# Output projection as seven block products for eight, and a gating summed in PSUM: one Trainium2 core

## The chip, the core and the metric

One of the eight cores of a Trainium2 chip runs the kernel. A core has a matrix engine (TensorE, PE in the profile, with PEld for its weight loads), a vector engine (VectorE, DVE), a scalar engine (ScalarE, ACT), a general engine (GpSimd, POOL) and a sync engine (SyncE, SP), which here issues every transfer between DRAM and the on-chip memory SBUF. TensorE writes its sums into PSUM, eight banks of 512 float32 columns per partition; VectorE and ScalarE read them there. Each engine works through its own instructions in a fixed order and waits on semaphores for the others.

The metric is the device time of one execution in microseconds, the median of several runs. The profiled execution is one more run, with the hardware profiler on.

## What is computed

One layer of a streaming encoder, for 2048 prompt tokens and 32 sample tokens (2080 rows of 1024 float32 numbers). Cut to what matters:

```python
h = jnp.einsum('bsd,de->bse', x, w_in)
u, v, ga, bv, bg, gb = jnp.split(h, ...)          # six pieces of 512 columns
u = jax.nn.gelu(u, approximate=False)
v = layer_norm(jax.nn.gelu(v, approximate=False), a_ln_g, a_ln_b)
y_a = u * spatial_gating(v, a_ws, a_bias) * jax.nn.silu(ga)
a = bv * jax.nn.sigmoid(bg)
c, new_hist = depthwise_causal_conv(conv_hist, a, b_conv_w, b_conv_b)   # 31 taps
y_b = jax.nn.silu(layer_norm(c, b_ln_g, b_ln_b)) * jax.nn.silu(gb)
y = jnp.einsum('bse,ed->bsd', jnp.concatenate([y_a, y_b], axis=-1), w_out)
x_new = layer_norm(ALPHA * x + y, post_ln_g, post_ln_b)
```

Spatial gating mixes positions: for each of 8 heads and each chunk of 128 tokens, a lower triangular 128 x 128 matrix is multiplied with the 64 channels of that head in v, and a bias is added.

## The kernel before

**Numbers in two parts.** TensorE is fed with fp32r, a 4-byte type that keeps fewer bits than float32. Every operand is therefore split: `hi` is the value cast to fp32r (ScalarE) and `lo` is the value minus `hi` (a subtraction on VectorE, `tt`, or on GpSimd, `gtt`). A product is then three matmuls, hi·hi, hi·lo and lo·hi, added in PSUM.

**Stages.** The tokens form four groups of 512; group 1 holds the 32 sample tokens as well. Two passes `p` of two groups each run over the input projection in steps: first `v` of the pass's first group (`mm_v`, lines 293 to 295), then `bg` and `bv`, `v` of the second group, `u`, `ga` and `gb` (`mm_f`, lines 266 and 269). A schedule clock `T0` counts 1 for a `v` step and 2 for the others, 192 units in all (`TEND`). A list planner orders each engine's instructions by priority; `when(t)` sets the priority of what follows, `at(t, ...)` hangs work on the step that begins at unit t. Weights come step by step: `load_w` four steps ahead, `split_w` up to three steps ahead, its low half on GpSimd.

**Spatial gating** (`spat`, lines 496 to 514). For two chunks of v at once, the 128 columns of two chunks' 64 channels are the weights, and `wt`, which holds the high and low part of a head's matrix side by side (256 columns), is the moving operand. Two matmuls (lines 507 and 508) with the high and the low part of v add into a PSUM area of 2 x 128 columns per head. The two halves are then added: ScalarE copies the first to `S` (line 513), VectorE adds the second (line 514, helper line 58). Each group takes 32 such matmuls and the sample 16, 144 in all.

**Convolution and its layer norm.** 31 taps on VectorE (helper line 61, tile `c`), two channel blocks at a time; `ln_chain` follows with column sums on TensorE (`colsum`, lines 378 and 379). For the last group they run into the output phase. The gated results y go to DRAM (`Yd`).

**Output projection.** `load_wo` reads the 16 tiles of w_out (8 k-blocks x 2 halves of 512 columns) and splits them, low parts on VectorE. Then come units of 256 tokens in the order 0, 1, 2, 3, sample, 4, 5, 6, 7. `load_y` reads y of a unit and splits it (ScalarE line 611, GpSimd), `load_r` reads x. `o_tile` makes a tile of 128 tokens: for each half of 512 columns 8 k-blocks x 3 matmuls (lines 659 to 661), then VectorE computes ALPHA·x + product from PSUM and takes statistics; the last tile's second half is cut into two pieces of 256. `finish` normalises: aggregate, a power on GpSimd, four multiplications with addition on VectorE, and the store. `o_sample` treats the 32 sample tokens with high and low part stacked as 64 weight columns.

Of the kernel before, what the change touches and what calls it, by code (L numbers as in the profile page):

```python
# [40 lines left out]
def hymba_step_kernel(ctx, tc, xT, xn, xs_n, wall, wsT, abias, vecs, avec, post, cache,  # L41
                      y_p, y_s, nc_p, nc_s, nav):

# [187 lines left out]
    def setup_hi():  # L231
        nc.scalar.copy(wt[:, :, 0, :], setup["wm"])
# [141 lines left out]
    def colsum(g, hl, nm):  # L374
        r = []
        for b, (c0, w) in enumerate(blocks(g)):
            p = ps.tile([P, W], F32, name=f"{nm}{g}_{b}", tag="c", bufs=2)
# [1 line left out]
            nc.tensor.matmul(p[:, :w], ones, hl[1][:, c0 : c0 + w], start=False, stop=True)
# [83 lines left out]
    def ev_v(g, res):  # L463
# [32 lines left out]
        def spat(u, pr, two):  # L496
# [3 lines left out]
            if (u, pr, two) == (0, 0, 0):  # L500
                S[g] = sb.tile([P, 4, WMAX], F32, name=f"S{g}", tag="S", bufs=2)
            p = bank(f"sp{g}_{u}_{pr}_{two}")
            for q in range(2):
# [3 lines left out]
                nc.tensor.matmul(o, hi, wt[:m, h], start=True, stop=False)  # L507
                nc.tensor.matmul(o, lo, wt[:m, h], start=False, stop=True)  # L508
            p4 = p.rearrange("p (q a b) -> p q a b", q=2, a=2)
            for j, (_, c0, _) in enumerate(ch):  # L510
                r = slice(64 * j, 64 * j + 64)
                d = S[g][64 * two : 64 * two + 64, pr : pr + 2, c0 : c0 + m]
                nc.scalar.copy(d, p4[r, :, 0, :m])  # L513
# [311 lines left out]
```

## Time and profile before

| what | value |
|---|---|
| time, median of 3 runs | 783.99 us (783.91 to 786.16) |
| the profiled execution, whole | 786.06 us |
| its span, first to last instruction | 784.2 us |
| TensorE busy | 764.3 us, 97% |
| VectorE busy | 627.7 us, 80% |
| ScalarE busy | 274.0 us, 35% |
| GpSimd busy | 260.5 us, 33% |
| transfers | 79.12 MB, mean 101 GB/s |
| matmuls and weight loads | 3799 of each |

How to read the profile: a row of the groups view has the line, the engine, the operation, the tile written and those read, the shapes (for a matmul rows*columns of the weights, then partitions x columns of the moving operand), the count, then busy microseconds and mean nanoseconds of one, then the engine's idle time just before and what ended it. A helper's line stands for all that call it: line 58 is every `tt`, 61 every `stt`, 64 every `gtt`, 67 every activation. A row of the timeline has start and length in us, and in brackets the idle time before. Matmuls overlap, so the slot of one is the distance between two starts, not its length.

### The profile page before, as it was taken

How to read it: one execution, taken by the hardware profiler on the slowest of the kernel's cores; microseconds unless marked ns; L12 is line 12 of the kernel's file. 1: busy time of each engine (PE TensorE's matmuls, PEld its weight loads, DVE VectorE, ACT ScalarE, POOL GpSimd, SP SyncE). 2: the span in 40 equal slices, each digit the busy share in tenths (PEclk: the TensorE clock that was granted, in tenths of full speed). 3: DMA queues.
4: the chain of work that ended last, by engine and by line, in shares of the span. 5: the costliest groups of instructions: out<-in, count | busy, mean ns of one | idle time of the engine just before them, and what ended most of it. 6: DMA issues, size and time to landing. Idle time of an engine off the chain costs nothing.

```text
span 784.2 us, 10387 instructions
## 1 busy us (share of the span) xinstructions
PE 764.3 (97%) x3799; PEld 640.6 (82%) x3799; DVE 627.7 (80%) x986; ACT 274.0 (35%) x499; POOL 260.5 (33%) x204
## 2 busy tenths in 40 slices
PE   8999999999999999999899999999989999899996
PEld 6799998799889998888688888888878888688885
DVE  5339999882799999965999996899999987955455
ACT  6562222353562234376312343551350124011100
POOL 2652122343313339451213343221213322243320
PEclk9999999999999999999999999999999999999998
DMA  9621112211125327411211311124542244354411
GB/s 296 234 67 43 41 41 52 87 53 42 37 65 172 123 81 210 114 40 43 82 53 58 95 40 54 41 94 161 176 146 70 82 150 152 141 182 161 147 54 54
DMA packets 45474, 79.12 MB, mean 101 GB/s; under 512 B 7152, under 2 KB 16496, under 8 KB 45296
## 3 DMA queue, kind: packets, MB, share of 16 engines
q1 hardware_dynamic: 45424, 78.46, 31.3%
q8 instruction: 30, 0.49, 0.3%
q14 instruction: 20, 0.16, 0.1%
HBM read 61.21 MB, written 17.23 MB: 100 GB/s over the span
## 4 chain that ended last, share of the span: by engine, by line
PE 92%; DVE 3%; ACT 2%; DMA 1%; issue 1%; POOL 0%; SPq 0%; DVEq 0%; ACTq 0%; POOLq 0%
PE f L266 37%; PE f L269 18%; PE o L659 8%; PE o L660 8%; PE o L661 8%; PE t L295 4%; PE t L294 4%; PE t L293 4%; PE sp L507 1%; DVE r L61 1%; PE sp L508 1%; DMA xr<-in_xT_dram 0%; DVE ls L406 0%; ACT A L67 0%; DVE gb L58 0%
## 5 line engine op out<-in xcount | busy, mean ns | idle before, releaser
L266 PE MATMUL f<-xs,wh 128*128 128x512 f32 (+1 forms) x1600 | 369.6, 352 | 5.3 <-DVE S L58 3.3
L61 DVE SCALAR_TENSOR_TENSOR c<-A,vec,c 128x512 f32<-128x512 f32 x464 | 319.3, 749 | 2.5 <-ACT c L67 0.6
L266 PEld LDWEIGHTS f<-xs,wh 128*128 128x128 f32 x1600 | 271.7, 189 | 48.0 <-issue 5.9
L64 POOL TENSOR_TENSOR wl<-wr,wh 128x512 fp32r<-128x512 f32 x104 | 138.6, 1335 | 320.5 <-ACT wh L145 311.1
L269 PE MATMUL f<-xs,wl 128*128 128x512 f32 (+1 forms) x800 | 214.2, 351 | 0.0
L269 PEld LDWEIGHTS f<-xs,wl 128*128 128x128 f32 x800 | 140.7, 188 | 20.4 <-issue 0.2
L145 ACT CAST wh<-wr 128x512 fp32r<-128x512 f32 x112 | 69.2, 620 | 237.1 <-PE f L266 139.5
L659 PE MATMUL o<-wo,yh 128*128 128x512 f32 (+1 forms) x264 | 103.9, 394 | 4.7 <-ACT yh L611 4.7
L660 PE MATMUL o<-wo,yh 128*128 128x512 f32 (+1 forms) x264 | 103.4, 392 | 0.0
L661 PE MATMUL o<-wo,yl 128*128 128x512 f32 (+1 forms) x264 | 97.5, 387 | 0.0
L64 POOL TENSOR_TENSOR yl<-yr,yh 128x512 fp32r<-128x512 f32 x32 | 44.9, 1411 | 83.4 <-ACT yh L611 82.2
L659 PEld LDWEIGHTS o<-wo,yh 128*128 128x128 f32 x264 | 50.6, 192 | 16.5 <-ACT yh L611 5.6
L660 PEld LDWEIGHTS o<-wo,yh 128*128 128x128 f32 x264 | 50.7, 192 | 10.7
L661 PEld LDWEIGHTS o<-wo,yl 128*128 128x128 f32 x264 | 50.0, 189 | 11.0
L611 ACT CAST yh<-yr 128x512 fp32r<-128x512 f32 x32 | 19.6, 621 | 106.9 <-PE o L660 81.4
L61 DVE SCALAR_TENSOR_TENSOR r<-r,o 128x512 f32<-128x512 f32 (+1 forms) x33 | 21.6, 666 | 42.1 <-PE o L661 42.1
L58 DVE TENSOR_TENSOR S<-sp,S 64x256 f32<-64x256 f32 (+1 forms) x68 | 27.8, 409 | 26.9 <-ACT S L513 25.2
L294 PE MATMUL t<-wl,xs 128*128 128x512 f32 x128 | 49.3, 395 | 0.0
L293 PE MATMUL t<-wh,xs 128*128 128x512 f32 x128 | 47.7, 394 | 1.4 <-ACT xs L185 1.4
L295 PE MATMUL t<-wh,xs 128*128 128x512 f32 x128 | 48.4, 397 | 0.0
L64 POOL TENSOR_TENSOR xs<-xr,xs 128x512 fp32r<-128x512 f32 (+1 forms) x24 | 31.4, 1323 | 28.3 <-ACT xs L165 28.3
L64 POOL TENSOR_TENSOR or<-or,mhalf 128x1 f32<-128x1 f32 x16 | 16.0, 1000 | 72.4 <-DVE or L639 72.2
(109 smaller groups left out, 677.7 us busy)
## 6 DMA issues: line engine op xcount, KB each, us to landing
wr<-in_wall_dram SPq DMA_DIRECT2D x112, 256.0 KB, 2.6
yr<-yd SPq DMA_DIRECT2D x64, 128.0 KB, 2.2
r<-in_xn_dram SPq DMA_DIRECT2D x16, 512.0 KB, 4.5
out_dram<-r SPq DMA_DIRECT2D x15, 512.0 KB, 2.6
xr<-in_xT_dram SPq DMA_DIRECT2D x23, 256.0 KB, 4.1
wor<-in_wall_dram SPq DMA_DIRECT2D x16, 256.0 KB, 2.8
yd<-S SPq DMA_DIRECT2D x12, 256.0 KB, 2.6
yd<-gb SPq DMA_DIRECT2D x12, 256.0 KB, 2.1
```

The costliest lines, as they stand in the source:

```text
L58: nc.vector.tensor_tensor(out, a, b, op=op)
L61: nc.vector.scalar_tensor_tensor(out, a, s, b, op0=op0, op1=op1)
L64: nc.gpsimd.tensor_tensor(out, a, b, op=op)
L145: nc.scalar.copy(hi, r)
L266: nc.tensor.matmul(pt[b][:, :w], hk, xsp[g, k][:, part, c0 : c0 + w], start=(k == 0 and part == 0), stop=False)
L269: nc.tensor.matmul(pt[b][:, :w], lk, xsp[g, k][:, 0, c0 : c0 + w], start=False, stop=(k == NK - 1))
L293: nc.tensor.matmul(pt[t][:m], hi[:, c0 : c0 + m], wh, start=st, stop=False)
L294: nc.tensor.matmul(pt[t][:m], hi[:, c0 : c0 + m], wl, start=False, stop=False)
L295: nc.tensor.matmul(pt[t][:m], lo[:, c0 : c0 + m], wh, start=False, stop=en)
L659: nc.tensor.matmul(p, hi, wh, start=(k == 0), stop=False)
L660: nc.tensor.matmul(p, hi, wl, start=False, stop=False)
L661: nc.tensor.matmul(p, lo, wh, start=False, stop=(k == NK - 1))
```

## The change

Three things change.

1. **Spatial gating in PSUM.** `wt` becomes two tiles, high and low. `spat` now takes four heads of one kind (`two`) into one bank of 4 x 128 columns and adds three matmuls of 128 columns per head there: hi·high, hi·low, lo·high. ScalarE copies the result to `S`; the addition on VectorE is gone, as is the fourth product lo·low.

```diff
-        def spat(u, pr, two):
+        def spat(u, two):
...
-                o = p[:w, 256 * q : 256 * q + 256]
-                nc.tensor.matmul(o, hi, wt[:m, h], start=True, stop=False)
-                nc.tensor.matmul(o, lo, wt[:m, h], start=False, stop=True)
...
+                o = p[:w, P * pr : P * pr + P]
+                for m3, (l, r) in enumerate(((hi, 0), (hi, 1), (lo, 0))):
+                    nc.tensor.matmul(o, l, wt[r][:m, h], start=(pr + m3 == 0), stop=(m3 == 2),
+                                     skip_group_check=True)
...
-                nc.scalar.copy(d, p4[r, :, 0, :m])
-                tt(d, p4[r, :, 1, :m], d, ADD)
+                nc.scalar.copy(S[g][64 * two : 64 * two + 64, :, c0 : c0 + m], p3[r, :, :m])
```

2. **Sums of w_out blocks.** With w_out as 2 x 2 blocks of 512 x 512 (B11, B12, B21, B22), `wo_sums` makes T1 = B12 - B11, T3 = B22 - B12, T2 = B22 - T1 and T4 = B21 - T2 on GpSimd, splits them and stores both parts in DRAM (`Td`). It is called eight times during the first pass, at units 24, 30, 36, 42, 70, 74, 78 and 82.

```diff
+    def wo_sums(kk, c):
...
+                nc.sync.dma_start(b[i, dh], wo_rows(4 * i + kk, dh)[:, cs])
+        gtt(b[0, 0], b[0, 1], b[0, 0], SUB)
+        gtt(b[0, 1], b[1, 1], b[0, 1], SUB)
+        gtt(b[1, 1], b[1, 1], b[0, 0], SUB)
+        gtt(b[1, 0], b[1, 0], b[1, 1], SUB)
+        for j, (n, t) in enumerate(((1, b[0, 0]), (3, b[0, 1]), (2, b[1, 1]), (4, b[1, 0]))):
+            hl = sb.tile([P, 2, 256], F32R, name=f"to{kk}{c}_{n}", tag="v" + "hl"[j % 2], bufs=VB)
+            nc.scalar.copy(hl[:, 0], t)
+            gtt(hl[:, 1], t, f(hl[:, 0]), SUB)
+            nc.sync.dma_start(Td[n, kk][:, :, cs], f(hl))
```

3. **The output phase.** Its order is now 0, 1, sample, 2, 3, 4, 5, 6, 7. Units 0 and 1 and the sample are computed as before. Units 2 to 7 (1536 tokens) use Winograd's form of Strassen's scheme on 2 x 2 blocks: the two tiles of 128 tokens and the two halves of k give A11, A12, A21, A22, VectorE makes S1 = A21 + A22, S2 = S1 - A11, S3 = A11 - A21 and S4 = A12 - S2, and seven products of 12 matmuls replace eight. Partial sums stay in three PSUM banks, A, B and C, that are read after each product and added to by a later one. `mm` chains all these matmuls in the order written. Every low part of y (`YDVE = ()`) and every second one of w_out is made on GpSimd. The layer norm of the last group (`late`) is cut into six stages that are put between the products. `load_y(0)` comes 13 units before the end of the input projection, w_out is loaded half by half, and T1 to T4 come back through `load_t`.

```diff
+    def mm(out, l, r, start, stop):
+        with tc.issue_after(order["mm"].ins):
+            order["mm"] = nc.tensor.matmul(out, l, r, start=start, stop=stop, skip_group_check=True)
...
+        (tt if k % 2 else gtt)(t[:, 1, :W], r, f(t[:, 0, :W]), SUB)
...
+    PRODUCTS = [("A11", "B11", "A"), ("A12", "B21", "B"), ("S2", "T2", "A"), ("S3", "T3", "C"),
+                ("S1", "T1", "A"), ("A22", "T4", "C"), ("S4", "B22", "A")]
...
+    def y_block(u, n):
...
+            tt(s1, a21, a22, ADD)
+            tt(a21, a11, a21, SUB)
+            tt(a11, s1, a11, SUB)
+            tt(a12, a12, a11, SUB)
...
+        nc.scalar.copy(hl[0], raw)
+        (tt if n in YDVE else gtt)(hl[1], raw, f(hl[0]), SUB)
...
+    def o_product(u, j, t0, final):
...
+        parts = [slice(0, 256), slice(256, W)] if final and j == 6 else [slice(0, W)]
+        for n, cs in enumerate(parts):
...
+            for kk in range(4):
+                wh, wl = wo[wn, kk]
+                for m, (l, w) in enumerate(((hi, wh), (hi, wl), (lo, wh))):
+                    mm(q, l[:, kk], w[:, cs], opens and kk + m == 0, kk == 3 and m == 2)
...
+            if j in (0, 2, 3, 6):
+                stt(r[t][:, c], r[t][:, c], ALPHA, q)
+            else:
+                tt(r[t][:, c], r[t][:, c], q, ADD)
...
+            if j in (1, 4, 5, 6):
+                nc.vector.bn_stats(ost[t][:, dh + n, :], r[t][:, c])
```

`finish` has a second form for all prompt tiles but the last: a small VectorE step for minus mean times scale, then ScalarE, VectorE and GpSimd one after another over the whole row of 1024.

```diff
+        if parts["out"] == [slice(0, D)] and m == P:
+            nm = sb.tile([P, 1], F32, name=f"on{tag}", tag="on1", bufs=4)
+            stt(nm, mv[:, 0:1], -1.0, r1, op0=MUL, op1=MUL)
+            act(r, r, AF.Identity, bias=nm, scale=r1)
+            tt(r, r, pgb[:, 0], MUL)
+            gtt(r, r, pgb[:, 1], ADD)
```

In the planning of the Strassen units, blocks of y are prepared up to five products ahead:

```diff
+            while ready < len(blocks_y) and ready - len(used) < 5:
+                v, n = blocks_y[ready]
+                if (v, "A11") not in yraw:
+                    when(t - 11 + j)
+                    load_yraw(v)
+                when(t + j - 8)
+                y_block(v, n)
+                ready += 1
+            o_product(u, j, t + j, u == units[-1])
+            stages(t + j, LATE.get((u, j), 0))
```

More of the change, by code (lines that the diff above doesn't have):

```diff
@@ L437, in run @@
                 lambda: (sw(0, 1, 2, 3), gates()),
-            )
+            ]
+            if g == 3:
+                late.extend(fns)
+            else:
+                chain(h, *fns)
         run()
@@ L546, in ev_v @@
         )
-        units = [(u, pr, two) for u in range(3 if five else 2) for pr in (0, 2) for two in range(2)]
+        units = [(u, two) for u in range(3 if five else 2) for two in range(2)]
         for j, a in enumerate(units):
-            at(h + 6 + 2 * j // 2 + (4 if a[0] else 0), lambda a=a: spat(*a))
-        at(h + 6 + len(units) + 4, spat_affine)
+            at(h + 6 + 2 * j + (4 if a[0] else 0), lambda a=a: spat(*a))
+        at(h + 6 + 2 * len(units) + 4, spat_affine)
     def gated(g, e, i):
@@ L677, in o_sample @@
                 for x in range(2):
-                    nc.tensor.matmul(p[: 2 * NS], both, wo[k, dh][:, x, :W],
-                                     start=(k == 0 and x == 0), stop=(k == NK - 1 and x == 1))
+                    mm(p[: 2 * NS], both, wo[f"B{1 + k // 4}{1 + dh}", k % 4][x],
+                       k == 0 and x == 0, k == NK - 1 and x == 1)
             s = slice(W * dh, W * dh + W)
             stt(r[:, s], r[:, s], ALPHA, p[:NS])
-            e = work(f"ro{dh}")[:NS, :W]
+            e = sb.tile([P, W], F32, name=f"ro{dh}", tag="wr", bufs=4)[:NS]
             nc.scalar.copy(e, p[NS : 2 * NS])
@@ new lines, in hymba_step_kernel @@
+    YDVE = ()
+    def o_product(u, j, t0, final):
+        yn, wn, grp = PRODUCTS[j]
+        if j in (0, 1, 3):
+            psum[grp] = bank(f"o{grp}{u}")
+        if j == 0:
+            for t in range(2):
+                ost[t] = sb.tile([P, 3, 6], F32, name=f"ost{u}_{t}", tag="ost", bufs=4)
+        hi, lo = Y[u, yn]
+        r = R[u]
+        parts = [slice(0, 256), slice(256, W)] if final and j == 6 else [slice(0, W)]
+        for n, cs in enumerate(parts):
+            when(t0 + n / 2)
+            q = psum[grp][:, cs]
+            opens = j in (0, 1, 3)
+            for kk in range(4):
+                wh, wl = wo[wn, kk]
+                for m, (l, w) in enumerate(((hi, wh), (hi, wl), (lo, wh))):
+                    mm(q, l[:, kk], w[:, cs], opens and kk + m == 0, kk == 3 and m == 2)
+            when(t0 - 12)
+            t, dh = ((0, 0), (0, 0), (1, 0), (1, 1), (1, 1), (1, 0), (0, 1))[j]
+            c = slice(W * dh + cs.start, W * dh + cs.stop)
+            if j in (0, 2, 3, 6):
+                stt(r[t][:, c], r[t][:, c], ALPHA, q)
+            else:
+                tt(r[t][:, c], r[t][:, c], q, ADD)
+            when(t0 + 1 + n / 2)
+            if j in (1, 4, 5, 6):
+                nc.vector.bn_stats(ost[t][:, dh + n, :], r[t][:, c])
+        if j in (5, 6):
+            split = final and j == 6
+            out = [slice(0, W), slice(W, W + W // 2), slice(W + W // 2, D)] if split else [slice(0, D)]
+            row = 256 * u + P * t
+            finish(r[t], P, {"st": ost[t], "n": 2 + split, "out": out}, y_p[row : row + P],
+                   f"{u}_{t}")
@@ L699, in hymba_step_kernel @@
     at(30, lambda: nc.sync.dma_start(pgb, bcast(post, P, 2 * D)))
+    for j in range(8):
+        at((24 + 6 * j) if j < 4 else (54 + 4 * j), lambda j=j: after_w(wo_sums, j // 2, j % 2))
     for k in range(8):
```

178 lines of the change are left out of this document (127 added, 51 removed).

## The prediction

> **What bounds the kernel now.** I read the page first (span, busy shares, chain), then the groups with shapes kept apart, the waits of TensorE, the windows around them, and the timeline at both ends of the output projection.
>
> ```profile
> span 784.2 us, 10387 instructions
> PE 764.3 (97%) x3799; PEld 640.6 (82%) x3799; DVE 627.7 (80%) x986; ACT 274.0 (35%) x499; POOL 260.5 (33%) x204
> ...
> GB/s 296 234 67 43 41 41 52 87 53 42 37 65 172 123 81 210 114 40 43 82 53 58 95 40 54 41 94 161 176 146 70 82 150 152 141 182 161 147 54 54
> ```
>
> TensorE (PE) is busy 764 of 784 us, so a matmul more or less is a gain or loss of its full slot, wherever it stands. The 20 us that it isn't busy are a start, an end, and three stops:
>
> ```profile
> 376.64 1.16 PE L266 MATMUL f<-xs,wh 128*128 128x512 f32 x2 [3.34 <-DVE S L58]
> 584.88 0.80 PE L659 MATMUL o<-wo,yh 128*128 128x512 f32 x1 [1.96 <-ACT yh L611]
> 686.36 0.50 PE L659 MATMUL o<-wo,yh 128*128 128x512 f32 x1 [2.75 <-ACT yh L611]
> 370.00:380.00 10.00, 6.66 (x27) 5.39 (x26) 9.78 (x17) 6.02 (x15) 1.67 (x1) 0.83 0.36 138
> 390.00:400.00 10.00, 10.00 (x44) 8.11 (x44) 8.68 (x14) 2.78 (x4) 2.43 (x2) 1.00 0.21 52
> 585.00:595.00 10.00, 10.00 (x37) 8.16 (x38) 10.00 (x15) 2.42 (x5) 5.33 (x3) 0.83 0.40 124
> 686.00:696.00 10.00, 9.64 (x35) 7.76 (x36) 6.16 (x7) 2.49 (x5) 7.93 (x6) 0.83 0.70 225
> ```
>
> The bracket is the idle time and who ended it; in the window rows PE's time and matmul count come first, the granted clock third from the end. After each stop the clock is 0.83 over ten microseconds: 37 and 35 matmuls where 44 fit, 7 and about 8 slots lost. So the stops cost 3.34+1.5 (estimate, by the other two), 1.96+1.6 and 2.75+1.9: 13 us in all.
>
> **The slots.** From the chain of waits, and the first and last of 48 matmuls of 256 columns in the last tile:
>
> ```profile
> 630.73 0.46 PE o L661 x2
> 571.82 0.93 PE f L266 x4
> 771.22 0.28 PE L659 MATMUL o<-wo,yh 128*128 128x256 f32 x1
> 776.76 0.28 PE L661 MATMUL o<-wo,yl 128*128 128x256 f32 x1
> L507 PEld LDWEIGHTS sp<-wt,vh 128*128 128x128 f32 x64 | 11.1, 188 | 1.0 <-DVE A L58 0.3
> L507 PEld LDWEIGHTS sp<-wt,vh 32*64 32x64 f32 x8 | 0.9, 129 | 0.6
> ```
>
> 512 columns take 0.231 us (0.93/4), 256 columns 5.54/47 = 0.118. A weight load of 128 columns lasts 59 ns longer than one of 64, so 0.92 ns a column, and 128 columns occupy the loader about 0.118 us (an estimate from these two rows). That equals the 256-column slot.
>
> **Strassen: removed matmuls.** A block product is 128 tokens x 512 x 512 for both token halves: 4 k-blocks x 3 (hi·hi, hi·lo, lo·hi) = 12 matmuls. Six units of 256 tokens go from 8 to 7 products: 6 x 12 = 72 matmuls of 0.231 = **-16.6 us**. Units 0 and 1 and the sample keep theirs. With no bound hiding it, the gain is whole if nothing else becomes late.
>
> **Spatial gating: 144 wide matmuls become 216 narrow ones.** Before, 4 groups x 32 + 16 for the sample, 256 columns: 144 x 0.118 = 17.0 us. After, 4 x 48 + 24 = 216 of 128 columns, each with its own weight load. No row shows a moving operand under 256 columns in this 4-byte type. Lower end: by columns alone 0.231/4 = 0.058, 12.5 us (-4.5). Upper end: the dearest matmul of the trace, 0.231, 49.9 us (+32.9). I take 0.118, the weight load, which must pass once per matmul: 25.5, so **+8.5 us**.
>
> The Trainium skill, "TensorE: Matmul & The Clock Gate", section "Back-to-back issue gap", gives about 81 ns per matmul at 128 columns for a stream with weight loads. By it the edit costs 17.5 - 17.0 = +0.5, not +8.5 (an estimate from that page); no run here shows it yet.
>
> **What the gating takes from VectorE and ScalarE.**
>
> ```profile
> L58 DVE TENSOR_TENSOR S<-sp,S 64x256 f32<-64x256 f32 x64 | 27.0, 422 | 26.8 <-ACT S L513 25.2
> L513 ACT COPY S<-sp 64x256 f32<-64x256 f32 x64 | 23.4, 366 | 20.0 <-PE sp L508 12.6 <-DVE S L58 5.3
> L379 PE MATMUL mu<-lr,ones x5: 287/389/394, 203.2 to 633.1; 128*128 128x512 f32 x3, 128*128 128x272 f32 x2
> ```
>
> All 27 us of adds go, and ScalarE does 32 copies of twice the width for 64. VectorE isn't the bound, so this is worth only what it unblocks: the 376 us stop waits for just such an add (a PSUM bank held by it). I book **-4.8**; 0 if another VectorE step holds the next bank instead (VectorE is busy 9.8 of those 10 us).
>
> **Sums of w_out blocks.**
>
> ```profile
> L64 POOL TENSOR_TENSOR wl<-wr,wh 128x512 fp32r<-128x512 f32 x104 | 138.6, 1335 | 320.5 <-ACT wh L145 311.1 <-ACT S L513 4.8 <-ACT ls L67 2.4
> 50.00:100.00 50.00, 49.94 (x320) 45.57 (x319) 43.60 (x72) 16.05 (x36) 12.87 (x11) 1.00 0.14 43
> 200.00:250.00 50.00, 50.00 (x303) 43.35 (x302) 46.58 (x71) 24.68 (x46) 13.37 (x10) 1.00 0.24 75
> ```
>
> Eight calls, each 8 GpSimd (POOL) steps of 256 columns (half of 1.335, an estimate), 4 casts, 4 loads and 4 stores: 43 us of GpSimd, 64 DMAs on SP's queue. They lie where GpSimd has about 37 of 50 us free. Queued behind them are the low halves of w, split up to three steps (about 17 us) ahead, and behind a store that waits for its sum, the loads of w, four steps ahead. Cost **0**; if a call blocks longer than that lead, PE waits microsecond for microsecond.
>
> **The start of the output phase.** y of unit 0 is loaded 13 schedule units early, so the 585 us stop loses its named cause. But the order of matmuls is now fixed, and the eight w_out tiles of the first half are needed one per 0.69 us; half their low parts move to GpSimd at 1.335 instead of 0.719. I book half, **-1.8**. The 686 us stop stood behind the sample, which now comes after unit 1: **-4.6**, 0 at worst. The layer norm of the last group has its sums at fixed places in PE's order, about 52 us in (224 matmuls of units 0, 1 and the sample), 635 us; the last such sum started at 633.1 before (the third row gives first and last start), with more VectorE work ahead of them. Cost 0; if the convolution is later, PE stands.
>
> **The hand-over.** The sums come back as 16 tiles of 512 KB, 8 MB. T3 is issued after unit 0's matmuls (96 x 0.231 = 22 us in), T2 after unit 1's (44 us), T1 waits for the sample's last use of B12, and T1 is needed at product 4 of unit 2 (52 + 4 x 2.77 = 63 us). So from 44 to 63 us T2 and T1 (4 MB), unit 1's stores and y of unit 3 (1 MB each) move: 6 MB in 19 us, 316 GB/s, where the highest slice of the page has 296. At 296 they take 20.3 us, 1 to 2 more. Cost 0 to 10 (T4's 2 MB in the same stretch); I take **+2**, the rate's own answer.
>
> **The steady Strassen units.** PE needs 84 x 0.231 = 19.4 us per unit.
>
> ```profile
> L64 POOL TENSOR_TENSOR yl<-yr,yh 128x512 fp32r<-128x512 f32 x32 | 44.9, 1411 | 83.4 <-ACT yh L611 82.2
> L64 POOL TENSOR_TENSOR or<-or,mhalf 128x1 f32<-128x1 f32 x16 | 16.0, 1000 | 72.4 <-DVE or L639 72.2
> L58 DVE TENSOR_TENSOR wo<-wor,wo 128x512 fp32r<-128x512 f32 x16 | 11.3, 719 | 0.1
> L61 DVE SCALAR_TENSOR_TENSOR r<-r,o 128x512 f32<-128x512 f32 x31 | 20.8, 682 | 38.8 <-PE o L661 38.8
> L664 DVE BATCH_NORM_STATS2 ost<-r 128x6 f32<-128x512 f32 x31 | 21.0, 688 | 0.6
> L58 DVE TENSOR_TENSOR wt<-wm,wt 128x1024 fp32r<-128x1024 f32 x1 | 1.2, 1226 | 0.1
> L232 ACT CAST wt<-wm 128x1024 fp32r<-128x1024 f32 x1 | 1.0, 1045 | 0.0
> ```
>
> VectorE: 7 reads of PSUM x 0.68, 4 statistics x 0.69, 4 block sums x 0.72, 2 multiplies x 1.23, about 1 of small steps: 13.9 us, hidden. GpSimd: 7 splits x 1.41, 2 powers x 1.0, 2 adds of 1024 x 2.67 (twice 1.335): **17.2 of 19.4**, hidden with little room. New waits: three PSUM banks are each reopened two products after they are read, so VectorE has one product, 2.77 us, to read a bank; behind PE's wait stands its whole fixed order. 0 to 6 us over six units; I take **+3**.
>
> **The tail.**
>
> ```profile
> 777.08 0.42 DVE L61 SCALAR_TENSOR_TENSOR r<-r,o 128x256 f32<-128x256 f32 x1 [1.96 <-PE o L661]
> 779.66 1.53 DVE L61 SCALAR_TENSOR_TENSOR r<-r,or,pgb 128x512 f32<-128x512 f32 x3
> out_dram<-r SPq DMA_DIRECT2D x15, 512.0 KB, 2.6
> ```
>
> The last tile keeps its short end: matmuls done at 777.0, span over 7.2 later. But the other half of unit 7, done one product (2.8 us) before, ends by ScalarE 1.05, VectorE 1.23 and GpSimd 2.67 after its statistics (0.68+0.69+0.35) and power (1.0), then its store (about 2.6): 10.3 plus hand-offs, against VectorE's work for the last tile. Between 0 and +5; **+2.5**.
>
> **Sum:** -16.6 + 8.5 - 4.8 - 1.8 - 4.6 + 2 + 3 + 2.5 = **-11.8 us**. The profiled run took 786.06 us for a span of 784.2; the median shown is 783.99. The span would be 772.4, the same run 774.3; from the median I forecast **772.2 us**.
>
> **Rivals.**
> *Narrow matmuls are dear (slower).* Place: 216 gating matmuls. If one costs as much as a 512-column one, 216 x (0.231-0.118) = +24.4: 796.6 us. It decides from 0.173 us each (0.118 + 11.8/216). For it: the shapes of the trace stop at 256 columns, so no row denies it. Against: from 512 to 256 columns the slot halves exactly (0.231, 0.118), with no sign of a dearer rate.
> *Narrow matmuls are cheap.* At 0.058, 13.0 less: 759.2. For it: wide slots go by columns exactly. Against: the loader's 0.118. By the 81 ns of the Trainium skill's page cited above, "TensorE: Matmul & The Clock Gate", it would be 764.2 (an estimate).
> *GpSimd sets the pace of the Strassen units.* Between power and add of one tile stand a VectorE step, ScalarE and VectorE (0.16+1.05+1.23, some 2.9 with hand-offs). If GpSimd idles there twice a unit, it needs 23.0 us against 19.4: 21.6 over six units, less a lead of up to five blocks (13.9): 7.7 to 21.6. With 10, most of the lead being there: 782, no change.
> The Trainium skill's "GPSIMD Engine Reference", section 3.1, says to keep elementwise work on VectorE, measured 1.96 times faster. The trace agrees (1411 against 719 ns, 1.96), and this rule speaks against giving GpSimd the splits.
> *It doesn't do what it says* (the planner puts other work between, so PE stops at each product) is the upper end of the +3.
>
> **How the numbers follow.** Forecast (764 to 780) 0.50; cheap 0.13 (755 to 764); GpSimd's pace 0.17 (780 to 794); dear 0.20 (from 784 up). About 0.3% is what a measurement of this kernel can tell from no change: faster means under 781.6, slower over 786.4. Faster 0.50 + 0.13 + 0.06 of GpSimd's case = 0.69; same 0.06; slower 0.20 + 0.05 = 0.25. The range 758 to 796 leaves out the lowest part of the cheap case (0.04) and the upper half of the dear one (0.10). The forecast's own range is 764 to 780.
>
> **What would show it.** The start-to-start of the new gating matmuls: 0.118, 0.058 or 0.231. The matmul count of the output phase, 728 for 800. No idle of PE named after S at the first stop. PE's clock at 1.00 through units 2 to 7, and a unit in 19.4 us; if longer, the releaser (POOL: its pace; DVE r: the banks; DMA t: the sums late). I am wrong if the gating slot is over 0.17, or if the last product of a unit waits for a GpSimd split.

## The result

The changed kernel took 805.06 us (median of 4 runs, 802.8 to 805.96), beside 785.08 us (783.91 to 787.47) for the kernel before on the same chip: a ratio of 1.0246, 95% interval 1.0211 to 1.0281. It is **slower by 2.5%**; 772.2 us was forecast, so the sign was wrong, and the time lies above the range.

The first lines of the page after:

```profile
span 801.1 us, 10703 instructions
PE 765.4 (96%) x3787; PEld 637.6 (80%) x3787; DVE 636.7 (79%) x937; ACT 309.6 (39%) x531; POOL 385.1 (48%) x309
```

TensorE is as busy as before (765.4 for 764.3 us), with fewer wide matmuls: what it saved came back in narrow matmuls and in slower ones. The span grew by 16.9 us. GpSimd (POOL) has 125 us more work. Where the time went is read from windows, before and then after. Columns: stretch and its length, then busy time (and count) of PE, PEld, DVE, ACT and POOL, granted clock, DMA share, GB/s.

```profile
210.00:220.00 10.00, 10.00 (x55) 7.18 (x53) 9.18 (x17) 5.76 (x12) 3.50 (x2) 1.00 0.12 34
220.00:230.00 10.00, 10.00 (x63) 8.91 (x63) 9.94 (x14) 5.92 (x10) 1.29 (x1) 1.00 0.28 83
230.00:240.00 10.00, 10.00 (x64) 9.10 (x64) 10.00 (x15) 4.76 (x9) 2.58 (x2) 1.00 0.31 105
...
650.00:777.00 127.00, 124.25 (x554) 99.84 (x552) 81.60 (x124) 17.25 (x27) 36.12 (x30) 0.99 0.36 125
```

```profile
210.00:220.00 10.00, 10.00 (x44) 6.94 (x43) 8.58 (x11) 3.39 (x7) 1.82 (x2) 0.86 0.14 34
220.00:230.00 10.00, 10.00 (x43) 6.77 (x42) 7.67 (x8) 6.71 (x11) 1.72 (x2) 0.84 0.15 52
230.00:240.00 10.00, 10.00 (x53) 9.09 (x52) 10.00 (x18) 1.53 (x4) 7.45 (x5) 0.79 0.34 106
...
595.00:647.00 52.00, 52.00 (x226) 40.40 (x225) 50.40 (x84) 13.11 (x20) 21.71 (x16) 1.00 0.52 167
647.00:790.00 143.00, 124.61 (x519) 98.90 (x518) 119.12 (x157) 46.12 (x63) 93.01 (x62) 0.95 0.41 143
```

Two places. **The front:** from 210 to 240 us PE is busy without a gap, yet makes 140 matmuls for 182, and its clock, 1.00 before, is 0.79 to 0.86. The first matmul of the output phase starts at 594.95 us for 584.88: +10.1. **The Strassen units**, 647 to 790 us: their 504 matmuls of 0.231 us need 116.4 us and take 143. The output phase as a whole takes 195.2 us with 728 matmuls, 191.9 with 800 before: +3.3, where -16.6 and the old stops' end should show. **The tail:** last matmul to the end of the span 10.9 us for 7.4: +3.5. The three make the 16.9.

PE's timeline after shows what each place is made of (start, length, in brackets the idle time before and who ended it):

```profile
52.09 0.28 PE L541 MATMUL sp<-wth,vh 128*128 128x128 f32 x1
...
52.98 0.28 PE L541 MATMUL sp<-wth,vl 128*128 128x128 f32 x1
...
213.91 0.27 PE L541 MATMUL sp<-wth,vl 32*64 32x128 f32 x1
214.11 0.50 PE L271 MATMUL f<-xs,wl 128*128 128x512 f32 x1
...
214.74 0.39 PE L271 MATMUL f<-xs,wl 128*128 128x272 f32 x1
215.06 0.27 PE L541 MATMUL sp<-wtl,vh 32*64 32x128 f32 x1
...
319.50 0.79 PE L295 MATMUL t<-wh,xs 128*128 128x512 f32 x1 [3.09 <-ACT gb L69]
...
657.51 0.80 PE L629 MATMUL oA<-t,yh_S 128*128 128x512 f32 x1 [4.43 <-DVE r L63]
```

The new gating matmuls of full size follow each other in 0.111 us (8 slots from 52.09 to 52.98): they are not dear. The sample's, with 32x64 weights, stand singly between wide ones, and each change costs: 0.20 us from a sample's to a wide one, 0.32 from 272 columns to a sample's, where 272 columns take 0.123 (0.231 x 272/512). At 657.51 PE has waited 4.43 us for VectorE's read of bank A. PE's longest waits behind 590 us, in us, times, longest:

```profile
PE oA L629 <- DVE r L63: 9.8, 5, 4.4
PE oA L629 <- DVE r L60: 2.8, 1, 2.8
PE oA L629 <- ACT yh_S L783: 2.6, 2, 2.1
PE oA L629 <- DVE on L63: 2.3, 1, 2.3
```

Nearly all stand at the reopening of bank A. Of the two that name ScalarE's cast `yh_S`, the longer one, 2.1 us, leads back to VectorE too: the cast waited 1.68 us for the block sum `yr`, which took 2.85. And this is VectorE, then GpSimd, ahead of the first stop:

```profile
651.22 1.21 DVE L60 TENSOR_TENSOR r<-r,pgb 128x1024 f32<-128x1024 f32 x1
652.35 1.75 DVE L60 TENSOR_TENSOR yr<-yr 128x512 f32<-128x512 f32 x1
654.04 2.81 DVE L60 TENSOR_TENSOR rs<-rs,ro 32x512 f32<-32x512 f32 x1
656.78 0.67 DVE L63 SCALAR_TENSOR_TENSOR r<-r,oA 128x512 f32<-128x512 f32 x1
```

```profile
651.40 2.17 POOL L66 TENSOR_TENSOR yl_S<-yr,yh_S 128x512 fp32r<-128x512 f32 x1 [4.48 <-ACT yh_S L783]
653.53 2.78 POOL L66 TENSOR_TENSOR r<-r,pgb 128x1024 f32<-128x1024 f32 x1
```

The subtraction `yr` and the sample's addition `rs` take 1.75 and 2.81 us, and end 0.53 and 0.54 us after a GpSimd step ends (653.57 and 656.31). Rows of single tiles over 647 to 790 us show it for the whole phase (min/median/max ns):

```profile
L63 DVE SCALAR_TENSOR_TENSOR on<-omv,or x12: 151/1070/1272, 647.0 to 789.9; 128x1 f32<-128x1 f32 x12
L60 DVE TENSOR_TENSOR yr<-ys,yr x5: 627/2853/2880, 673.4 to 760.8; 128x512 f32<-128x512 f32 x5
L63 DVE SCALAR_TENSOR_TENSOR r<-r,oA x18: 420/673/689, 656.8 to 788.3; 128x512 f32<-128x512 f32 x17, 128x256 f32<-128x256 f32 x1
```

A step on one column takes 0.15 us at its shortest and 1.07 at the median, a block sum 0.63 and 2.85. The reads of PSUM, with one operand in SBUF, stay at 0.67 to 0.69 from the median up (the 0.42 is the one of 256 columns). So the theory: **VectorE's steps on two SBUF operands stand still while GpSimd runs**, the bank reads queued behind them come late, and PE has one product (2.77 us) of slack. The Trainium skill's "SBUF — State Buffer", section "Who interferes with whom", states such a rule: a VectorE instruction with two SBUF inputs contends with a GpSimd instruction that reads SBUF, because its second input comes through a shared read interface, and the shared pair of ports is an exclusive lock; with at most one SBUF input, outside VectorE's two-port modes, it does not contend. The trace agrees in both halves (2.85 us for 0.63; 0.67 to 0.69).

The second stop, 4.3 us up to 683.3, looks otherwise. VectorE works from 670.1 to 683.1 us without a gap, and ahead of the read of bank A stand steps of the last group's layer norm:

```profile
670.13 3.35 DVE L436 RECIPROCAL ls<-ls 128x512 f32<-128x512 f32 x1 [1.06 <-ACT ls L69]
...
675.14 3.33 DVE L60 TENSOR_TENSOR A<-A,ls 128x512 f32<-128x512 f32 x4
...
681.28 1.27 DVE L60 TENSOR_TENSOR gb<-gb,A 128x512 f32<-128x512 f32 x1
682.47 0.67 DVE L63 SCALAR_TENSOR_TENSOR r<-r,oA 128x512 f32<-128x512 f32 x1
```

These three rows take 7.95 us; GpSimd's holds lengthen the steps of this stretch by some 2 us only (an estimate, from the shortest steps of the same kind). So a second cause stands beside the first: VectorE's other work in the same fixed order. By unit of 256 tokens, units 2 to 6 (columns as above):

```profile
647.40:673.50 26.10, 21.67 (x88) 17.24 (x87) 24.73 (x29) 10.11 (x15) 12.86 (x8) 0.93 0.72 257
673.50:701.80 28.30, 22.10 (x86) 17.26 (x85) 24.92 (x33) 11.77 (x16) 15.85 (x12) 0.88 0.49 161
701.80:728.70 26.90, 21.42 (x86) 16.52 (x85) 24.58 (x30) 6.66 (x10) 21.92 (x14) 0.94 0.53 180
728.70:749.70 21.00, 20.04 (x85) 15.75 (x84) 16.43 (x23) 6.45 (x9) 16.79 (x12) 0.99 0.28 96
749.70:770.10 20.40, 19.59 (x86) 15.68 (x85) 15.82 (x22) 6.62 (x9) 15.88 (x12) 1.00 0.13 52
```

The loss lies in units 2 to 4, where VectorE is busy for 24.6 to 24.9 us each. In unit 2 some 18 us of that are the last group's layer norm and the sample's rows, in unit 3 6.5 us; in unit 4 none is left. Units 5 and 6 take 21.0 and 20.4 us, near the 19.4 that PE needs.

### The profile page after: what moved, and what is told of

The parts are those of the page before. It is cut to its first block, busy times and chain, and to the rows that moved or that the text cites. A ratio compares the mean times of both kernels' runs of the same rounds, so it can differ in the third digit from the quotient of the medians.

```text
span 801.1 us, 10703 instructions
## 1 busy us (share of the span) xinstructions
PE 765.4 (96%) x3787; PEld 637.6 (80%) x3787; DVE 636.7 (79%) x937; ACT 309.6 (39%) x531; POOL 385.1 (48%) x309
## 4 chain that ended last, share of the span: by engine, by line
PE 73%; DVE 11%; DMA 6%; POOL 4%; issue 3%; SPq 1%; ACT 1%; POOLq 0%; DVEq 0%; ACTq 0%
PE f L268 33%; PE f L271 16%; PE oA L629 5%; PE t L296 3%; PE t L297 3%; PE t L295 3%; DVE c L63 3%; PE oC L629 3%; PE o L629 2%; PE sp L541 2%; DVE yr L60 2%; DMA xr<-in_xT_dram 2%; DMA td<-to 1%; DVE r L60 1%; DVE r L63 1%
## 5 line engine op out<-in xcount | busy, mean ns | idle before, releaser
L60 DVE TENSOR_TENSOR S<-S,u 128x512 f32<-128x512 f32 (+1 forms) x16 | 15.4, 989 | 48.9 <-ACT u L69 48.9
L66 POOL TENSOR_TENSOR r<-r,pgb 128x1024 f32<-128x1024 f32 x15 | 38.6, 2576 | 14.6 <-DVE r L60 9.3
L629 PE MATMUL oA<-t,yh_S 128*128 128x512 f32 x96 | 33.3, 430 | 11.7 <-DVE r L63 9.3
L66 POOL TENSOR_TENSOR to<-bo,to 128x256 fp32r<-128x256 f32 x32 | 27.1, 852 | 18.7 <-ACT to L328 18.7
L66 POOL TENSOR_TENSOR yl_S<-yr,yh_S 128x512 fp32r<-128x512 f32 x18 | 27.6, 1540 | 16.5 <-ACT yh_S L783 15.9
L66 POOL TENSOR_TENSOR yl_A<-yr,yh_A 128x512 fp32r<-128x512 f32 x18 | 26.6, 1481 | 17.8 <-ACT yh_A L783 9.8
L69 ACT ACTIVATE r<-r,on,or 128x1024 f32<-128x1024 f32 x15 | 18.6, 1243 | 42.1 <-DVE on L63 42.1
L629 PEld LDWEIGHTS oA<-t,yh_S 128*128 128x128 f32 x96 | 19.5, 208 | 17.9 <-issue 8.9
L295 PEld LDWEIGHTS t<-wh,xs 128*128 128x128 f32 x128 | 24.7, 194 | 10.8 <-ACT gb L69 3.5
L66 POOL TENSOR_TENSOR vl<-gv,vh 128x512 fp32r<-128x512 f32 (+1 forms) x17 | 22.8, 1360 | 21.3 <-ACT vh L526 21.3
```

Of the source, the lines that this page charges most:

```text
L60: nc.vector.tensor_tensor(out, a, b, op=op)
L66: nc.gpsimd.tensor_tensor(out, a, b, op=op)
L69: nc.scalar.activation(out, in_, func, bias=bias, scale=scale)
L295: nc.tensor.matmul(pt[t][:m], hi[:, c0 : c0 + m], wh, start=st, stop=False)
L629: order["mm"] = nc.tensor.matmul(out, l, r, start=start, stop=stop, skip_group_check=True)
```

## Experiments

The table holds every run. *Ratio* is to the kernel before on the same chip. The last three columns come from the one profiled execution, whose time can differ from the median by a few us (789.97 for 794.29 in `sample_grouped`). *Mark* is the start of one ScalarE step, the first eviction of v in the second pass, against 322.60 us before. *Stops* sums the distances of over 0.65 us between two matmul starts behind 590 us, less the first one's slot; *half clock* sums the smaller surpluses there (0.43 us for 0.231).

| run | us | ratio (95%) | mark | stops | half clock |
|---|---|---|---|---|---|
| before | | 1 | 0 | 2.9 | 1.4 |
| the change | 805.1 | 1.0246 (1.0211–1.0281) | +15.2 | 20.0 | 5.5 |
| gating_only | 792.0 | 1.0063 (1.0035–1.0091) | +12.2 | 5.0 | 3.1 |
| strassen_only | 796.5 | 1.0117 (1.0097–1.0137) | +7.9 | 19.7 | 5.4 |
| sample_grouped | 794.3 | 1.0076 (1.0051–1.0100) | +3.8 | 19.5 | 4.5 |
| sums_late | 790.4 | 1.0054 (1.0030–1.0079) | +1.6 | 19.7 | 5.8 |
| grouped_no_low | 778.4 | 0.9888 (0.9855–0.9921) | +3.6 | 7.1 | 2.3 |
| grouped_no_low_dummy | 793.6 | 1.0079 (1.0049–1.0109) | +6.9 | 19.6 | 6.4 |
| old_finish | 796.9 | 1.0134 (1.0109–1.0159) | +14.3 | 19.0 | 3.8 |
| grouped_ydve | 794.6 | 1.0102 (1.0066–1.0138) | +7.6 | 18.4 | 5.7 |
| late_spread | 791.4 | 1.0070 (1.0045–1.0095) | +7.2 | 16.5 | 6.1 |
| paired | 793.5 | 1.0075 (1.0047–1.0104) | +6.8 | 16.5 | 4.5 |
| skew | 789.6 | 1.0048 (1.0028–1.0067) | +8.0 | 15.0 | 5.8 |
| skew_ydve | 792.1 | 1.0071 (1.0047–1.0096) | +8.4 | 17.1 | 4.2 |
| skew_ydve_all | 792.6 | 1.0078 (1.0047–1.0109) | +8.5 | 17.9 | 4.9 |
| skew_dveadd | 786.8 | 1.0005 (0.9983–1.0026) | +5.7 | 13.7 | 5.3 |
| skew_dveadd_y2 | 789.3 | 1.0025 (1.0002–1.0047) | +5.8 | 18.9 | 2.3 |
| skew_dveadd_sl | 782.1 | 0.9938 (0.9917–0.9958) | +0.7 | 13.9 | 5.1 |
| skew_best | **780.2** | **0.9911 (0.9891–0.9932)** | +0.2 | 14.2 | 2.5 |
| skew_best_s | 786.7 | 0.9994 (0.9977–1.0012) | +2.5 | 18.9 | 3.9 |

### The front: each part alone

The kernel before with the new `spat` and its two `wt` tiles; and the changed kernel with the old ones.

> The kernel before with the new gating alone; the output projection is left in its old form. Theory (the sample's unit): the gating of full 128-row units costs nothing, the sample's 24 matmuls of 64 weight columns, laid singly between wide ones, cost some 10 us with the half clock behind them, and the stop of 4.8 us at 376 us is gone but a new one of 3.4 us stands at 320 us: slower than before by 8 to 11 us, about 793 to 796 us, no stops behind 600 us other than those of the kernel before. Rival (the stops of the Strassen units are the whole loss): within 2 us of the kernel before. Rival (my forecast's +8.5 for 72 more matmul slots spread over all groups): a lag that grows by 2 us in each of the four groups instead of at one place.

> The changed kernel with the old gating (two products per head, high and low weights side by side, the sum on VectorE). Theory: the front of the kernel runs as before, so the loss of some 10 us at 211 to 246 us is gone; the stops between 650 and 790 us stay at some 26 us in sum: 793 to 797 us, 8 to 12 us over the kernel before. Rival (the gating is the whole loss, Strassen gains its 16.6 us): 770 us. Rival (order of work of the front, moved by the sums of w_out blocks on GpSimd, is the cause of the front's loss): the front is still late by 5 us or more at 590 us.

The new gating alone costs 5 us. By evictions like the mark it is 3.9 us late at 207 us and 12.0 at 256 us, with the clock at half for 10.2 us between; the stop at 376 us, now gone, gives some 4.5 back. The time, 792.0, is a little below the expected 793 to 796. Strassen alone keeps its 25 us of stops and half clock, as expected, but not the clean front: the last rival of that run is true as well, the first matmul of the output phase starting at 590.50 us, 5.6 late. So the sample's matmuls aren't the whole front.

**The sample's 24 matmuls as a group**, ahead of a step's wide ones:

```diff
+            if u == 2:
+                when(T0[cur["h"]] - 3)
             for pr in range(4):
```

> The changed kernel, with the sample's 24 narrow gating matmuls mostly in two rows of their own ahead of a step's wide ones, instead of singly between them. Theory (each change between a narrow and a wide matmul costs some 0.3 to 0.4 us, and the slow clock comes from that stretch): the lag at 246 us falls from 12 to about 3 to 6 us and the time to 796 to 800 us. Rival (the narrow matmuls of 64 columns are dear by themselves, or the data that they wait for is late): the lag stays at 10 us or more, 804 to 806 us.

794.3 us, 10.8 less by the medians, 13 by the ratios: more than expected. The eviction that was 12.6 us late at 256 us is 7.6 late, the mark 3.8 for 15.2. The windows of this run, 220 to 240 us:

```profile
220.00:230.00 10.00, 10.00 (x64) 9.09 (x63) 8.49 (x12) 5.37 (x10) 9.43 (x8) 1.00 0.54 168
230.00:240.00 10.00, 10.00 (x65) 9.09 (x64) 8.55 (x9) 5.79 (x10) 6.49 (x8) 1.00 0.65 205
```

129 matmuls for 96 and the clock at 1.00. The same matmuls, in another order: it is the alternation that costs, by the changes and by the clock together; no run parts the two. The Trainium skill's "TensorEngine Tiling (Array Packing)", section "Key Properties", says that a change of the tiling mode drains TensorE; the 0.20 and 0.32 us at each change would fit that, and no run measured a drain by itself.

**The sums of w_out later**, the second half of the calls at units 122 to 134 for 70 to 82:

```diff
-        at((24 + 6 * j) if j < 4 else (54 + 4 * j), lambda j=j: ...
+        at((24 + 6 * j) if j < 4 else (106 + 4 * j), lambda j=j: ...
```

> The kernel with the sample's rows grouped (794.3 us), with the second half of the sums of w_out blocks moved from some 190 to 262 us to some 350 to 420 us, where the transfers are quiet. Theory (the sums' work on GpSimd and their transfers hold up the splits of x and of the weights at 300 to 320 us): the stops there (4 us) go, and the time falls by 3 to 6 us. Rival (that stop comes from the gating's new timing alone): the lag at 330 us stays, 792 to 796 us.

3.9 us less by the medians (the intervals of the ratios overlap; the pair `skew_dveadd` and `skew_dveadd_sl` below differs by this edit alone, on one chip, and there they don't). PE no longer waits between 290 and 340 us. In the run with the sample grouped it did:

```profile
PE t L296 <- POOL wl L66: 1.9, 1, 1.9
PE t L295 <- ACT gb L69: 1.4, 1, 1.4
```

GpSimd had 52.2 us of work between 180 and 265 us there, and has 29.7 now.

### The Strassen units: who holds VectorE

**GpSimd's subtractions taken away, and put back as work that nobody uses.** The low part of y in units 2 to 7 isn't made; the high part stands in for it in the matmuls. The second kernel adds:

```diff
+        gtt(hl[1], pgb[:, 0, :W]..., pgb[:, 1, :W]..., SUB)
         Y[u, n] = [hl[0], hl[0]]
```

> The kernel with the sample's matmuls in rows of their own (794.3 us), without the low part of the y blocks in units 2 to 7: the high part stands in its place in the third matmul of each three, so the matmuls stay and GpSimd loses 42 subtractions of some 1.3 us alone. The low part of y is left out of the result there. Theory (VectorE's bank reads come late because its steps on two SBUF operands stand still beside GpSimd): the stops of 21 us in units 2 to 7 fall to 3 to 9 us; 778 to 786 us. Rival (the order of the banks alone, one product between the last matmul into bank A and the next): the stops stay at 15 us or more, 790 to 795 us.

> As the run without the low part, but GpSimd makes the 42 subtractions all the same, on constant rows, into tiles that nobody reads. So no matmul and no VectorE step waits for a result of GpSimd's subtractions, and only the time in which both engines run is as in the kernel with the sample's rows grouped. The low part of y is left out of the result. Theory (VectorE is held while GpSimd runs): most of the stops are back, 12 to 20 us in sum, and the time is 788 to 795 us. Rival (GpSimd's results come late, its throughput is the limit): the stops are as few as without the subtractions, 778 to 786 us.

778.4 us without the subtractions and 793.6 with the unused ones, both on one chip: 15.2 us; stops 7.1, then 19.6 (the mark differs by 3.3 us between these two profiles, ahead of the stops). Over the six units VectorE is busy for 94.2 us in 153 steps, then for 108.1 us in 152. First the run without, then the run with them:

```profile
L63 DVE SCALAR_TENSOR_TENSOR on<-omv,or x11: 150/159/161, 672.8 to 762.8; 128x1 f32<-128x1 f32 x11
L60 DVE TENSOR_TENSOR yr<-ys,yr x5: 674/685/693, 643.5 to 718.7; 128x512 f32<-128x512 f32 x5
```

```profile
L63 DVE SCALAR_TENSOR_TENSOR on<-omv,or x12: 106/160/2346, 641.9 to 782.7; 128x1 f32<-128x1 f32 x12
L60 DVE TENSOR_TENSOR ys<-yr,yr x4: 673/694/2835, 662.2 to 720.2; 128x512 f32<-128x512 f32 x4
```

Without the subtractions the one-column step takes 0.16 us every time; with them up to 2.35. And the longest stop of the second run (4.3 us, ended at 702.2), VectorE and then GpSimd:

```profile
696.28 2.83 DVE L60 TENSOR_TENSOR ys<-yr,yr 128x512 f32<-128x512 f32 x1
...
701.43 0.63 DVE L63 SCALAR_TENSOR_TENSOR r<-r,oA 128x512 f32<-128x512 f32 x1
```

```profile
696.19 2.38 POOL L66 TENSOR_TENSOR r<-r,pgb 128x1024 f32<-128x1024 f32 x1
698.52 1.72 POOL L66 TENSOR_TENSOR yl_A<-pgb 128x512 fp32r<-128x512 f32 x1
```

By PE's waits no matmul waits for a y block in that run: all of them in the output phase end at VectorE or at the layer norm's sums (6.5 of the 19.6 us stand before those sums, 2.8 of the 7.1 without the subtractions). One link remains: the y tiles go round a ring of ten, which holds ten high parts in the first kernel and five pairs in the second, so ScalarE's casts waited for unused subtractions (31.8 us in all), of which 2.7 us reached VectorE. So it is GpSimd's activity, not the lateness of its results, that brings back most of these 12.5 us of stops. Where the 7 us left come from it doesn't show.

**Work moved between the two engines.** `if False:` in place of the new branch of `finish` (no GpSimd adds); `YDVE = ("A12", "S3", "A22")`; and the last four steps of the late layer norm spread over units 2 to 4 (unit 4's rows of x also take other tiles there):

```diff
-    LATE = {(1, 0): 1, (2, 1): 1, (2, 4): 1, (2, 5): 1, (2, 6): 1}
+    LATE = {(1, 0): 1, (2, 2): 1, (3, 0): 1, (3, 4): 1, (4, 1): 1}
```

> The changed kernel with the old layer norm of the output for all tiles: two pairs of VectorE steps in place of a step each on ScalarE, VectorE and GpSimd. GpSimd loses thirteen adds of 1024 columns (2.6 us each), VectorE gains some 2.5 us a tile. Theory (VectorE's steps on two SBUF operands stand still beside GpSimd): the stops become shorter, 3 to 10 us in sum, less what the longer VectorE work adds; 795 to 803 us, with fewer VectorE steps over twice their undisturbed length. Rival (the order of the banks alone sets the stops, VectorE being too busy): slower than the changed kernel by 5 us or more, since VectorE has 30 us more to do. Rival (GpSimd's own throughput sets the stops): 785 to 795 us.

> The kernel with the sample's rows grouped, and the low part of three of the seven y blocks of a unit (A12, S3, A22) on VectorE in place of GpSimd: GpSimd loses 18 subtractions of 1.3 us alone (more beside VectorE), VectorE gains 18 of 0.67 us alone. Theory (exclusive time of the two engines): the stops fall by 4 to 12 us, 783 to 790 us. Rival (VectorE is full by itself): the stops grow, 796 to 802 us.

> The kernel with the sample's rows grouped; the last four steps of the late layer norm of the last token group, which all lie in unit 2, are spread over units 2 to 4. Theory (VectorE held by GpSimd in every unit): only the stops of the first units move; the sum of the stops stays above 12 us and the time between 788 and 795 us. Rival (the late layer norm in unit 2 is what makes VectorE late): the stops of units 2 and 3 (some 13 us of 19) go, 780 to 785 us.

The old `finish` gains 8 us, but not by fewer stops (19.0 us; 3 to 10 were expected), and its stops are other ones: PE waits 8.1 us for the late layer norm's first sums, since VectorE ends the convolution at 649.5 us for 640.9, and 7.3 us for VectorE's reads of banks A and C. Three blocks on VectorE change nothing (a miss: 783 to 790 were expected). Spreading the late layer norm is worth 3 us at most, not 13, and the ratios don't differ; it takes none of its steps away, so it doesn't show what they cost.

### More slack at the banks

In `paired` the products of two units alternate; in `skew` a unit's second half alternates with the next one's first, with a third pair of banks, and the late layer norm's matmuls come later (in `paired`, unit 5's rows of x, in place of unit 7's, also take other tiles):

```diff
+    seq = sorted([(u, j) for u in units for j in range(7)], key=lambda a: 7 * a[0] + 2 * a[1])
```

> The kernel with the sample's rows grouped, and the products of two Strassen units taken in turn (unit 2's first, unit 3's first, unit 2's second, ...), with three banks for each unit; the late layer norm's last steps lie at each second product from the start. Between the last matmul into bank A and the first of the next product into it stand three products (8.3 us) for one. Theory (reads that are up to 5.5 us late): the stops at bank A go, at most 6 us of stops in sum remain, 776 to 784 us. Rival (GpSimd and VectorE together have too much to do, so that they fall behind for good): the stops move to the matmuls that wait for a y block's low part, and the time stays within 5 us of 794 us.

> The kernel with the sample's rows grouped, and each Strassen unit's second half taken in turn with the first half of the next (unit 3 begins after four products of unit 2, and so on), so that two products or more (5.5 us) stand between matmuls into one bank in the middle of the phase, with a third pair of banks; the late layer norm's step with matmuls lies four products later than in the run of pairs, where matmuls waited 8.7 us for it. GpSimd's and VectorE's work is unchanged. Theory (slack at the banks covers late reads; a limit by the two engines' exclusive time, some 22 us a unit, remains): stops of 6 to 14 us in sum, 780 to 788 us. Rival (the two engines fall behind for good): 790 to 795 us, with matmuls waiting for y blocks' low parts.

> As the run with units taken in turn by halves, and the low part of A12, S3 and A22 on VectorE. Exclusive time a unit: GpSimd 4 x 1.3 + 2 x 2.5 = 10.2 us, VectorE's steps on two SBUF operands 4 x 0.67 + 2 x 1.2 + 3 x 0.67 = 7.1 us, 17.3 us of 19.4. Theory: both limits are off, stops of 2 to 8 us in sum, 775 to 783 us. Rival (VectorE full): as slow as the run with units in turn alone, or slower, 785 to 792 us.

> As before, with the low parts of all seven blocks on VectorE: VectorE 8.4 us on one SBUF operand and 9.8 on two, 18.2 us of 19.4 a unit, GpSimd only the last adds (5 us). Theory: VectorE is nearly full, but GpSimd seldom holds it: 776 to 786 us. Rival (GpSimd's hold is not the matter, VectorE's own load is): 790 us or more.

Slack alone isn't the answer. Three products of it left 16.5 us of stops (at most 6 were expected): 9.4 for the late layer norm, the rest at late reads and once for a low part. The skewed order gives 4.7 us against the run with the sample grouped, less than expected, and the intervals of the ratios overlap. With three or seven blocks on VectorE the times, 792.1 and 792.6, are about those of the rivals, in which VectorE's own load is the limit: the theory's 775 to 786 was missed twice. One stop of 7.6 or 9.0 us stayed; in the latter run two GpSimd adds take 6.6 us there, and the two VectorE steps beside them, ahead of the bank read, 4.9. Hence the adds on VectorE:

```diff
-            gtt(r, r, pgb[:, 1], ADD)
+            (gtt if tag in ("0_0", "0_1", "1_0") else tt)(r, r, pgb[:, 1], ADD)
```

> As the run with units taken in turn by halves (789.6 us), with the last add of 1024 columns of the Strassen units' layer norm on VectorE (1.2 us) in place of GpSimd (2.5 to 3.3 us); all subtractions stay on GpSimd. A unit: VectorE 15.9 us, GpSimd 7 x 1.3 and two powers, 10.6 us; exclusive 7.5 + 10.6 = 18.1 of 19.4 us. Theory (VectorE is held longest by GpSimd's adds): the stops fall from 15 us to 3 to 9 us, 778 to 784 us. Rival (VectorE's own load): as slow as before or slower, 789 us or more.

> As the run with the adds on VectorE, and the low parts of A12 and A22 on VectorE too: VectorE 17.2 us, GpSimd 8 us, exclusive 16.8 us of 19.4 a unit. Theory (exclusive time): stops of 2 to 8 us, within 3 us of the run with the adds alone. Rival (VectorE full): 5 us slower than that run.

> The run with units in turn by halves and the adds on VectorE, and with the sums of w_out blocks moved to the quiet stretch. If both theories hold, the two gains add up: 772 to 780 us, faster than the kernel before. If the front's stop has another cause: as the run without the move.

The adds bring 2.8 us (6 to 12 were expected). More blocks on VectorE bring nothing, and their stops, 18.9 us for an expected 2 to 8, speak against the rule behind that forecast, that GpSimd's time and VectorE's two-operand steps need only fit into the unit together: 10.2 us are one stop at 715.7, ahead of which VectorE works from 704.6 to 715.6 us without a gap, some 3 us of it held (an estimate, from the shortest steps of the same kind), the rest its own work. The later sums add 4.7: the two gains do add up, to 782.1 us, above the 772 to 780 expected. There a stop of 4.8 us at 706 us was left: unit 5's rows of x are loaded at 700.5 and 702.8 us, behind unit 2's last store at 697.9, since the two units share a buffer; in `skew_best` they use the tiles that the layer norm frees (`u in (4, 5)` for `u in (4, 7)`). In `skew_best_s` the sample comes between units 0 and 1 as well.

> The run with units in turn by halves, adds on VectorE and sums in the quiet stretch (782.1 us), with the rows of units 4 and 5 (not 4 and 7) in the tiles that the layer norm frees, so that unit 5's rows need not wait until unit 2 is stored. Theory (the stop of 5.1 us at 706 us and 6.8 us of half clock come from these rows): 772 to 777 us. Rival (VectorE is late there anyway): 780 us or more.

> The same with the sample's output projection between units 0 and 1, not between unit 1 and unit 2. Theory (the sample's steps on two SBUF operands ahead of unit 2's first bank read make it late): the stop of 4.5 us and 3.4 us of half clock at 643 us go, 2 to 6 us faster than the run without this. Rival (the late layer norm's steps, or unit 1's last ones, take their place; VectorE is full with the convolution until 630 us): no faster, or slower by up to 5 us.

780.2 us, **0.9% faster than the kernel before** and 3.3% faster than the change by their ratios (0.9911/1.0246). The stop of 4.8 us went and half of the half clock, but smaller stops took its place (14.2 us for 13.9); 772 to 777 was missed, the time is the rival's (VectorE is late there anyway), and the gain over the run before it, 1.9 us, lies within the intervals. Moving the sample gave a stop of 8.6 us before the layer norm's sums: the rival was right. The phase of the Strassen units in `skew_best`, and PE's waits there:

```profile
640.00:768.00 128.00, 117.23 (x494) 93.04 (x494) 114.81 (x157) 41.19 (x57) 67.93 (x50) 0.97 0.40 136
```

```profile
PE oA L631 <- DVE r L63: 7.6, 3, 4.0
PE oC L631 <- DVE omv L704: 2.7, 3, 1.1
PE oA L631 <- DVE r L60: 1.8, 1, 1.8
```

VectorE is still 90% busy, and every wait of PE there is still for it.

## Why the prediction was wrong

- **Strassen, -16.6:** right as far as it went; 728 matmuls for 800, in slots of 0.231.
- **The steady Strassen units, the failing step.** "VectorE ... 13.9 us, hidden" summed undisturbed durations of a unit's own steps, and "I take +3" for the banks hung on it. Measured: 20.0 us of stops and 5.5 of half clock. Two things were missing from VectorE's sum. The first is held time: GpSimd's 17.2 us a unit were counted as hidden because nobody waits for GpSimd, but VectorE's steps on two SBUF operands stand still in them; the unused subtractions alone lengthened the same VectorE work from 94.2 to 108.1 us and the stops from 7.1 to 19.6. The second is the work that units 2 and 3 inherit, some 18 and 6.5 us of the late layer norm and the sample, which the prediction booked at 0. How the 25.5 us divide between the two no run shows. That GpSimd's 17.2 us and the two-operand steps (4 x 0.72 + 2 x 1.23 = 5.3 us) make 22.5 for a unit of 19.4 isn't the reason by itself: units 5 and 6 carry the same splits and adds and take 21.0 and 20.4 us, and the three runs planned at 16.8 to 18.1 us by this sum (`skew_ydve`, `skew_dveadd`, `skew_dveadd_y2`) kept 13.7 to 18.9 us of stops. The trace of before held the hint, in the shortest, median and longest of two of its groups, which the prediction didn't read:

```profile
L58 DVE TENSOR_TENSOR S<-S,u x16: 677/1258/1820, 168.7 to 503.1; 128x512 f32<-128x512 f32 x12, 128x544 f32<-128x544 f32 x4
L58 DVE TENSOR_TENSOR ls<-ls,ls x16: 645/702/1793, 167.1 to 642.9; 128x512 f32<-128x512 f32 x12, 128x544 f32<-128x544 f32 x4
```

  One and the same step takes 0.65 or 1.8 us: a median would have asked beside what.
- **Narrow gating matmuls, +8.5:** near in part, and in part by luck. Full units take 0.111 us a slot (0.118 taken; the cheap rival's 0.058 and 0.081 were not seen), which makes 4 x (48 x 0.111 - 32 x 0.118) = +6.2 us. The sample's 24, for which 0.9 us was booked, were laid singly between wide ones; most of the lag's growth from 3.9 to 12.0 us in `gating_only` is theirs, half clock included. That price was in the change of shape, of which I had no term. Both rivals on the slot's price, dear and cheap, missed this. By its time `gating_only` costs 5.0 us, where 8.5 - 4.8 = 3.7 was booked.
- **The stop at 376 us, -4.8:** gone, some 4.5 us. **Sums of w_out, 0:** wrong; the stop of 3.1 us at 319 us and its half clock are theirs, 3.9 us by `sums_late`.
- **585 us, -1.8, and 686 us, -4.6:** right; from 595 to 647 us PE is busy 52.00 of 52 us at clock 1.00.
- **Hand-over, +2:** nothing; no wait of PE ends at a load of the T tiles.
- **GpSimd sets the pace** as a rival had the right engine and the wrong path: it isn't its results that come late.
- **Tail, +2.5:** +3.5, and again two operands beside GpSimd: the last tile's two VectorE steps take 3.49 us together beside the other tile's GpSimd add:

```profile
792.67 3.49 DVE L63 SCALAR_TENSOR_TENSOR r<-r,omv,pgb 128x512 f32<-128x512 f32 x2
```

What stays open: the shares of held time and of inherited work in the 25.5 us (no run takes the late layer norm away from VectorE), and whether an order of VectorE's steps exists that removes the last 14 us of stops.

## What to carry to other kernels

Before work is moved to an engine that looks free, ask what it holds while it runs, not only who waits for it: look in the trace for one and the same VectorE step at very different lengths, and see what GpSimd did beside the long ones. Add to VectorE's sum the time in which it is held and the work that earlier stages leave to it; that GpSimd's time and VectorE's two-operand steps fit into a stage together was not enough here. Where PE reopens a PSUM bank one product after its last use, VectorE's longest stretch of work ahead of the read decides, not its mean load. And keep matmuls with small weights together; singly between wide ones they can cost several times their own slots.

## What was unexpected of the hardware

- TensorE's clock fell to half (10.2 us of it between 217 and 235 us) in a stretch in which PE shows no idle time at all, only alternating weight shapes; with the same matmuls grouped it stayed at 1.00. With the old gating's shapes in turn it fell for 3.4 us in `strassen_only` and not at all in the kernel before.
- A VectorE step on one column per partition took up to 2.35 us beside GpSimd, fifteen times its 0.16.
- GpSimd is held too: its 512-column subtraction `yl_S` took 1.26 us at its shortest in units 2 to 7 of the changed kernel and 2.32 at its longest; the one of 2.29 at 699.31 us ran beside a VectorE step of 1024 columns (`r`, 1.71 us) and one of 512 (`ys`, 1.20).
